# Second attention of a hybrid decoder layer: a branch product in two query halves, its last input kept on chip, and three moved or merged steps

## The chip, the cores and the metric

The kernel runs on one core of a Trainium2 chip. The metric is the device time of one execution in microseconds (us); the kernel before takes 1424.58 us, the median of three runs between 1424.15 and 1425.3. TensorE is called PE here, VectorE DVE, ScalarE ACT, GpSimd POOL, and SP is the engine whose queue issues nearly all DMAs of this kernel.

## What is computed

One layer with three parallel token mixers over 512 tokens and a model width of 1024:

```python
h = rms_norm(x);  u = h @ w_in                       # one combined projection
y_a = dsa_mixer(...)                                 # first attention (16 heads)
y_b = nsa_mixer(...)                                 # second attention (16 heads, two groups of 8)
y_c = ssd_mixer(...)                                 # state space mixer (2048 wide)
gates = sigmoid(mg)                                  # three gates per token and column
mix = gates[0]*(y_a @ w_br_dsa) + gates[1]*(y_b @ w_br_nsa) + gates[2]*(y_c @ w_br_ssd)
x = x + mix @ w_out
x = x + square(relu(rms_norm(x) @ w_ff1)) @ w_ff2
```

The second attention adds, for each query, a window part and a selected-blocks part (and a compressed part), each with its own softmax and gate. Everything is float32. A float32 product is computed as three matmuls of rounded operands: each operand is split into a high half (a rounded copy, made on ACT) and a low half (the operand less its high half, made on POOL or DVE), and `mm3` (L352) issues high x high, low x high and high x low.

## The kernel before

Two Python generators write the program. `main` (L1513) holds the attention and the state space mixer, `filler` (L577) holds the dense projections. `main` yields a cost, and the loop at its end lets `filler` emit about as much work; `main`'s instructions are emitted with a priority that is 4000 ahead (`HM`, L36). The order of each engine's queue is set when the program is built, from these priorities. So the attention's steps stand first wherever they are ready, and the projections fill TensorE between them. A generator that yields `None` waits for a flag in `done`.

The second attention (`nsa_units`, L987) runs 8 pairs of a query block b (128 queries) and a head group g in the order (3,0) (0,0) (2,0) (1,0) (3,1) (2,1) (1,1) (0,1). Each pair has two sets j of four heads and for each set a window unit and a selected-blocks unit, 32 units in all. A unit's scores are made by `a1` (L788) and exponentiated on ACT; `a2` (L812) takes 1/sum, multiplies it by the gate (L818) and scales four p tiles with it, three on DVE (L823) and the fourth on POOL (L821); `b1` (L825) transposes the p tiles, splits them and multiplies them with V into `pv`. At the end of a set ACT copies the lower part of `pv` (L856), DVE adds the two parts (L857), and SP writes the 256 rows by 128 queries to `y_d["b"]` in DRAM (L858).

`branches` (L1247) is the last part of the filler that runs beside this attention: the passes a0, a1, c0, c1, b0, b1 in this order. Each pass multiplies some row tiles of a mixer's result (128 rows by 512 queries, four in a0, a1, b0 and b1, eight in c0 and c1) with a branch weight, for eight column tiles m of the output. For a pass `load_y` (L709) reads each row tile from DRAM into a staging buffer (two exist), makes the high half on ACT (L715) and the low half on POOL (L716; in b1 on DVE), into a pool of four buffers: pool A for a0, B for a1 and b0, both for c0 and c1, and a pool C for b1. For each m, `load_g` (L1253) reads the gate tile, 128 by 512, 256 KB, into one of two buffers named `gld`; the product goes to one of two PSUM banks named `pj`; DVE multiplies it with the gate in place (L1329, or L1331 in c, where L1319 first multiplies the gate with a norm factor; in a0 L1326 writes `mix` at once); then `mix` takes it up, on POOL (L1332) in a1, c0, c1 and b0 and on DVE in b1. A gate buffer is free only after that addition, so a gate tile is loaded into it after the addition for m-2.

b1 is the last pass: rows 512 to 1023 of `y_d["b"]`, that is group g=1 of all four query blocks. It starts when the last unit is being emitted (flag `nsa5`), opens two column tiles with the two row tiles of set j=0, and waits for `nsa`, the attention's end, for the two row tiles of set j=1. After each column tile of b1, ACT and DVE make the halves `mixh`, `mixl` (L1334, L1335), on which the output product `w_out` (pass "wo") rests. Weights come in chunks of up to 128 by 1024 through `WS` (L104): three raw buffers (`RAWB`), six split ones (`NS`); the weight of a0, a1, b0 and b1 is one chunk of 128 by 512 for each m, that of c0 and c1 128 by 1024.

## Time and profile before

| | |
|---|---|
| median of three runs | 1424.58 us (1424.15 to 1425.3) |
| profiled execution, its own time | 1425.82 us |
| its span, first to last instruction | 1424.1 us |
| TensorE matmul busy | 1365.5 us (96%) |
| TensorE weight load busy | 1126.1 us (79%) |
| VectorE busy | 1044.6 us (73%) |
| ScalarE busy | 712.6 us (50%) |
| GpSimd busy | 347.0 us (24%) |
| mean granted TensorE clock | 0.987 |

The second attention runs from about 600 to 1010 us, the passes a0 to b1 from 749 to 1039 us, the output product from 1039 us on. A TensorE busy share near 100% doesn't mean that the engine is at its peak, since matmuls overlap; the spacing of starts is read beside it.

### The profile page before, as it was taken

The page shows a single profiled execution, that of the slowest core. Times are in us where ns is not written, and L with a number is a line of the kernel's source. Part 1 is how long each engine was busy: PE and PEld are TensorE (multiplying, and loading weights), DVE is VectorE, ACT ScalarE, POOL GpSimd, SP SyncE. Part 2 cuts the span into 40 slices and gives each one's busy share as a digit, 9 for nine tenths or more (in the row PEclk, how much of TensorE's full clock was granted, in tenths as well). Part 3 has the DMA queues.
Part 4 walks back from the last instruction along what each step waited for, and adds up shares of the span by engine and source line. Part 5 has one row for each costly group of instructions (what it writes and reads, how often), then busy time and mean ns, then how long its engine had stood idle before and what let it go on. Part 6 is the DMA issues. An engine that isn't in the chain of part 4 may idle for free.

```text
span 1424.1 us, 19720 instructions
## 1 busy us (share of the span) xinstructions
PE 1365.5 (96%) x6760; PEld 1126.1 (79%) x6760; DVE 1044.6 (73%) x1959; ACT 712.6 (50%) x1433; POOL 347.0 (24%) x294
## 2 busy tenths in 40 slices
PE   5989899999999999999999999999799999999998
PEld 4878688888877877788888867787579888888887
DVE  4599966798977665468568898888655777869841
ACT  5445245677666566455555544646433444443420
POOL 5454201111046576202003533524100000000000
PEclk9999899999999999999999999999999999999999
DMA  6236465544576778844326743424464433241221
GB/s 204 73 102 139 130 189 144 137 113 125 133 224 190 215 202 223 232 139 122 96 79 193 228 134 87 136 67 126 158 212 127 126 111 110 87 136 45 67 89 52
DMA packets 232097, 195.92 MB, mean 138 GB/s; under 512 B 17200, under 2 KB 183484, under 8 KB 231996
## 3 DMA queue, kind: packets, MB, share of 16 engines
q1 hardware_dynamic: 226524, 183.12, 44.3%
q0 software_dynamic: 4608, 8.39, 2.2%
q10 hardware_dynamic: 864, 3.15, 0.6%
q8 instruction: 53, 0.87, 0.3%
q14 instruction: 48, 0.39, 0.1%
HBM read 157.85 MB, written 36.77 MB: 137 GB/s over the span
## 4 chain that ended last, share of the span: by engine, by line
PE 71%; DVE 10%; DMA 7%; issue 4%; ACT 4%; POOL 2%; SPq 2%; DVEq 0%; ACTq 0%; POOLq 0%
PE pj L365 17%; PE pj L366 17%; PE pj L367 16%; PE sc L366 3%; PE sc L367 3%; PE sc L365 3%; PE pT L837 2%; PE sc L802 2%; PE sc L801 2%; PE pv L850 2%; PE pv L849 2%; DVE wlo L159 1%; DMA gld<-g_d 1%; SPq L525 1%; DMA E<-ac_d 1%
## 5 line engine op out<-in xcount | busy, mean ns | idle before, releaser
L158 ACT ACTIVATE whi<-wraw 128x1024 fp32r<-128x1024 f32 (+3 forms) x188 | 181.7, 975 | 210.8 <-PE pj L366 124.3
L159 DVE TENSOR_TENSOR wlo<-wraw,whi 128x1024 fp32r<-128x1024 f32 (+1 forms) x164 | 194.5, 1188 | 77.4 <-ACT whi L158 75.6
L365 PE MATMUL pj<-hTh,whi 128*128 128x512 f32 x384 | 154.9, 403 | 0.2 <-DVE cacc L732 0.2
L367 PE MATMUL pj<-hTh,wlo 128*128 128x512 f32 x384 | 153.5, 400 | 0.0
L366 PE MATMUL pj<-hTl,whi 128*128 128x512 f32 x384 | 153.3, 399 | 0.0
L365 PE MATMUL pj<-whi,hTh 128*128 128x512 f32 (+2 forms) x352 | 141.6, 404 | 8.3 <-DVE stk L435 3.2
L810 ACT ACTIVATE p<-p,nb,rs 128x256 f32<-128x256 f32 (+3 forms) x192 | 123.2, 645 | 50.6 <-DVE nb L808 50.6
L366 PE MATMUL pj<-wlo,hTh 128*128 128x512 f32 (+2 forms) x352 | 140.0, 398 | 0.8 <-POOL wlo L159 0.8
L367 PE MATMUL pj<-whi,hTl 128*128 128x512 f32 (+2 forms) x352 | 138.5, 394 | 0.0
L365 PE MATMUL pj<-yh,whi 128*128 128x512 f32 x256 | 103.0, 406 | 9.4 <-ACT yh L715 7.7
L366 PE MATMUL pj<-yl,whi 128*128 128x512 f32 x256 | 102.2, 399 | 0.4 <-DVE yl L716 0.4
L367 PE MATMUL pj<-yh,wlo 128*128 128x512 f32 x256 | 101.9, 399 | 0.0
L366 PE MATMUL pj<-h2l,whi 128*128 128x512 f32 (+1 forms) x256 | 96.3, 376 | 0.0
L367 PE MATMUL pj<-h2h,wlo 128*128 128x512 f32 (+1 forms) x256 | 96.2, 376 | 0.0
L365 PE MATMUL pj<-h2h,whi 128*128 128x512 f32 (+1 forms) x256 | 96.1, 376 | 0.0
L821 POOL TENSOR_TENSOR p<-p,rc 128x256 f32<-128x256 f32 (+3 forms) x48 | 38.2, 795 | 219.7 <-DVE rc L816 63.2
L365 PEld LDWEIGHTS pj<-whi,hTh 128*128 128x128 f32 x352 | 68.3, 194 | 22.5 <-issue 6.4
L365 PEld LDWEIGHTS pj<-hTh,whi 128*128 128x128 f32 x384 | 72.3, 188 | 16.4 <-issue 1.7
L367 PEld LDWEIGHTS pj<-hTh,wlo 128*128 128x128 f32 x384 | 72.2, 188 | 15.2 <-issue 1.2
L366 PEld LDWEIGHTS pj<-hTl,whi 128*128 128x128 f32 x384 | 72.3, 188 | 15.0 <-issue 1.7
L841 ACT ACTIVATE pth<-pT 128x512 fp32r<-128x512 f32 x95 | 55.0, 593 | 56.8 <-PE pT L837 54.8
L366 PEld LDWEIGHTS pj<-wlo,hTh 128*128 128x128 f32 x352 | 68.4, 194 | 14.9 <-issue 2.2
(357 smaller groups left out, 3372.9 us busy)
## 6 DMA issues: line engine op xcount, KB each, us to landing
wraw<-in_w_in_dram SPq DMA_DIRECT2D x84, 512.0 KB, 4.5
wraw<-in_w_ff_dram SPq DMA_DIRECT2D x40, 512.0 KB, 4.1
gld<-g_d SPq DMA_DIRECT2D x48, 256.0 KB, 3.3
qd<-in_w_ff_dram SPq DMA_DIRECT2D x24, 512.0 KB, 3.9
q_d<-qev SPq DMA_DIRECT2D x128, 64.0 KB, 2.6
qu<-q_d POOLq DMA_DIRECT2D x32, 256.0 KB, 3.7
E<-ac_d SPq DMA_DIRECT2D x16, 512.0 KB, 4.9
wraw<-in_w_br_ssd_dram SPq DMA_DIRECT2D x16, 512.0 KB, 3.8
```

What stands on the lines that cost most here:

```text
L158: act.activation(hi[:, :m], r[:, :m], AF.Copy)
L159: (pool if i < NP else dve).tensor_tensor(lo[:, :m], r[:, :m], f(hi[:, :m]), op=ALU.subtract)
L365: pe.matmul(o, lh, rh, start=first, stop=False)
L366: pe.matmul(o, lh, rl, start=False, stop=False)
L367: pe.matmul(o, ll, rh, start=False, stop=last)
L801: pe.matmul(s_[:, h % w, :n], u.q[:, h], kh[:, :n], start=True, stop=False)
L802: pe.matmul(s_[:, h % w, :n], u.q[:, h], kl[:, :n], start=False, stop=True)
L810: act.activation(u.p[h][:, :n], u.p[h][:, :n], AF.Exp, bias=u.nb[:, h:h + 1], scale=rs8[:, u.b, u.h0 + h:u.h0 + h + 1], accum_out=u.sm[:, ...
L821: pool.tensor_tensor(u.p[h][:, :n], u.p[h][:, :n], bc(rc[:, h:h + 1], [128, n]), op=ALU.mult)
L837: pe.transpose(pt[:, h], u.p[h][:, kb * 128:kb * 128 + 128], ident)
L841: act.activation(ph, ptf, AF.Copy)
L849: pe.matmul(o, vk, ph0, start=st, stop=False)
```

## The change

The branch weight of a is used in one pass of eight row tiles, with 128 by 1024 chunks. The weight of b comes in chunks of four row tiles by 256 columns (two m). The pass b1 takes only queries 256 to 511 (blocks 2 and 3), and starts while the seventh pair runs (flag `nsah`); a new pass b2 takes queries 0 to 255 with the same weights, which stay in their buffers. Queries 0 to 127 of b2 are the last pair's result: it is put from PSUM straight into b2's operand tiles `YH`, `YL` and goes to no DRAM. All low halves of y are made on DVE, and the fourth p tile of the second attention is scaled on ACT. The diff, cut to its core:

```diff
-SPL = {"a0": 1, "a1": 1, "c0": 1, "c1": 1, "b0": 1, "b1": 0}
...
-    P["br_a0"] = [plan_ch(A["w_br_dsa"], D, 128 * m, 0, 4) for m in range(8)]
-    P["br_a1"] = [plan_ch(A["w_br_dsa"], D, 128 * m, 4, 4) for m in range(8)]
+    P["br_a0"] = [plan_ch(A["w_br_dsa"], D, 128 * m) for m in range(8)]
...
-    P["br_b0"] = [plan_ch(A["w_br_nsa"], D, 128 * m, 0, 4) for m in range(8)]
-    P["br_b1"] = [plan_ch(A["w_br_nsa"], D, 128 * m, 4, 4) for m in range(8)]
+    for br, k0 in (("b0", 0), ("b1", 4)):
+        P["br_" + br] = [ws.add([(wcols(A["w_br_nsa"], D, k0, 4, 256 * m, 256), 256)], 4, 256) for m in range(4)]
...
-        (pool if SPL[br] else dve).tensor_tensor(l_, yr, f(h_), op=ALU.subtract)
+        dve.tensor_tensor(l_, yr, f(h_), op=ALU.subtract)
...
             if h == 3:
-                pool.tensor_tensor(u.p[h][:, :n], u.p[h][:, :n], bc(rc[:, h:h + 1], [128, n]), op=ALU.mult)
+                if u.gate is not None:
+                    act.activation(u.p[h][:, :n], u.p[h][:, :n], AF.Copy, scale=rc[:, h:h + 1])
+                else:
+                    pool.tensor_tensor(u.p[h][:, :n], u.p[h][:, :n], bc(rc[:, h:h + 1], [128, n]), op=ALU.mult)
...
+        if u.last and u.direct is not None:
+            yt = at.tile([64, 4, 128], F32, name="yt", bufs=YTB)
+            act.activation(yt.rearrange("p a b -> p (a b)"), o[64:128], AF.Copy)
+            yr, h_, l_ = u.direct
...
+            for e in range(2):
+                dve.tensor_tensor(yr[64 * e:64 * e + 64], o4[:, :, e], t4[:, :, e], op=ALU.add)
+            act.activation(h_, yr, AF.Copy)
+            dve.tensor_tensor(l_, yr, f(h_), op=ALU.subtract)
...
+        def half(g):
+            yield from g
+            done.add("nsah")
+
+        def direct(u, j):
+            done.add(f"nsaq{j}")
+            yield "yC"
+            u.direct = YC[j]
...
+                    if i == 7 and kind == "s":
+                        u.load = lambda u=u, j=j: direct(u, j)
+                    elif i == 6 and j == 1 and kind == "s":
+                        u.load = lambda i=i: half(cont(i + 1, cmp_c))
...
+        BR = ("a0", "c0", "c1", "b0", "b1", "b2")
+        KS = {"a0": (0, 8), "c0": (0, 8), "c1": (8, 8), "b0": (0, 4), "b1": (4, 4), "b2": (4, 4)}
+        COLS = {"b1": (256, 512), "b2": (0, 256)}
...
-                g_ = bp.tile([128, S], F32, name="gld", bufs=2)
-                nc.sync.dma_start(g_, g_d[(bi * 8 + m) * 128:(bi * 8 + m + 1) * 128])
+                c0, c1 = COLS.get(br, (0, S))
+                g_ = bp.tile([128, S], F32, name="gld", bufs=2)[:, :c1 - c0]
+                nc.sync.dma_start(g_, g_d[(bi * 8 + m) * 128:(bi * 8 + m + 1) * 128, c0:c1])
...
             if br == "a0":
-                Y = ya
-                Y1 = load("a1", range(4, 8), "B")
+                Y = ya + load("a0", range(4, 8), "B")
...
+            elif br == "b1":
+                while "nsah" not in done:
+                    yield None
+                yc = popen("yC")
+                YH = yc.tile([128, 4, S], F32R, name="yh2")
+                YL = yc.tile([128, 4, S], F32R, name="yl2")
+                load_b(256, 512)
...
+                yr = gp.tile([128, 2, 2, 128], F32, name="yr", tag="gt", bufs=TG)
...
+            elif br == "b2":
+                while "nsaq0" not in done:
+                    yield None
+                load_b(128, 256)
+                while "nsaq1" not in done:
+                    yield None
...
+                    if half:
+                        while "nsa" not in done:
+                            yield None
                     for m in range(BH):
...
                         for k in (2 * half, 2 * half + 1):
-                            mm3(pp[m], wh[:, k, :], wl[:, k, :], yh[k], yl[k], k == 0, k == 3)
+                            mm3(pp[m][:, :256], wh[:, k, ms], wl[:, k, ms], YH[:, k, 0:256], YL[:, k, 0:256], k == 0, k == 3)
...
+                            if k % 2:
+                                if k == 3 and m % 2 and br != "b1":
+                                    ws.free(wi)
+                                yield 6 * (c1 - c0) / 2.37
...
-                (dve if br == "b1" else pool).tensor_tensor(mix[:, m], mix[:, m], th, op=ALU.add)
-                if br == "b1":
+                (dve if br in ("b1", "b2") else pool).tensor_tensor(mx, mx, th, op=ALU.add)
+                if br == "b2":
                     act.activation(mixh[:, m], mix[:, m], AF.Copy, scale=0.5)
                     dve.scalar_tensor_tensor(mixl[:, m], mix[:, m], 0.5, f(mixh[:, m]), op0=ALU.mult, op1=ALU.subtract)
```

`load_b` reads the four row tiles of one query range in one or two DMAs and splits them on ACT and DVE. `mixh` and `mixl` are made in b2 for all 512 queries.

## Rows read from the trace of the kernel before

**Rows 1.** Busy time by stretch: PE, PEld, DVE, ACT, POOL (instructions), granted clock, DMA share, GB/s.
```profile
750.00:1001.00 251.00, 242.89 (x1239) 197.63 (x1238) 216.34 (x502) 134.80 (x302) 100.56 (x82) 1.00 0.47 139
1005.00:1020.00 15.00, 7.45 (x22) 4.92 (x23) 5.30 (x7) 2.77 (x5) 1.67 (x1) 0.77 0.35 107
1095.00:1110.00 15.00, 15.00 (x128) 15.00 (x127) 6.44 (x8) 5.83 (x8) 0.00 (x0) 1.00 0.81 287
```

**Rows 2.** Who TensorE waited for, 750 to 1001 us (largest): total, times, longest.
```profile
PE sc L801 <- DVE mx L803: 2.9, 6, 1.3
```

**Rows 3.** Timeline of TensorE at the attention's end: start, us, instruction, [idle before, releaser].
```profile
1001.15 0.39 PE L367 MATMUL pj<-yh,wlo 128*128 128x512 f32 x1
1016.35 1.22 PE L365 MATMUL pj<-yh,whi 128*128 128x512 f32 x2 [7.18 <-ACT yh L715]
1018.23 0.63 PE L365 MATMUL pj<-yh,whi 128*128 128x512 f32 x1
1018.65 0.63 PE L366 MATMUL pj<-yl,whi 128*128 128x512 f32 x1
1039.18 0.39 PE L367 MATMUL pj<-yh,wlo 128*128 128x512 f32 x1
```

**Rows 4.** The chain that ended last, 1003 to 1025 us: start, us, what.
```profile
1010.54 2.45 DMA yb_d<-yt
...
1013.01 2.64 DMA yr<-yb_d
...
1015.67 0.64 ACT yh L715
```

**Rows 5.** Gate tiles on two timelines: two SP issues, then three DVE instructions of one buffer.
```profile
1007.17 0.95 SPq L1258 DMA_DIRECT2D gld<-g_d  x1
...
1029.03 0.32 SPq L1258 DMA_DIRECT2D gld<-g_d  x1
...
1026.58 0.69 DVE L1329 SCALAR_TENSOR_TENSOR gld<-gld,pj 128x512 f32<-128x512 f32 x1 [0.86 <-DMA gld<-g_d]
...
1028.32 0.69 DVE L1332 TENSOR_TENSOR mixf<-mixf,gld 128x512 f32<-128x512 f32 x1
...
1033.04 0.68 DVE L1329 SCALAR_TENSOR_TENSOR gld<-gld,pj 128x512 f32<-128x512 f32 x1
```

**Rows 6.** A 256-column product on DVE, both operands in SBUF (timeline).
```profile
828.16 0.40 DVE L943 TENSOR_TENSOR pgt<-ct,gate 128x256 f32<-128x256 f32 x1
```

**Rows 7.** Groups of instructions, whole span: busy, mean ns, idle before and its releasers.
```profile
L716 POOL TENSOR_TENSOR yl<-yr,yh 128x512 fp32r<-128x512 f32 x28 | 40.1, 1441 | 26.6 <-ACT yh L715 24.8 <-DMA yr<-ya_d 1.6 <-DMA gld<-g_d 0.2
L1200 ACT ACTIVATE yev<-pT,gcol 128x128 f32<-128x128 f32 x64 | 17.9, 361 | 7.4 <-issue 7.1 <-PE pT L1197 0.3
L1334 ACT ACTIVATE mixh<-mixf 128x512 fp32r<-128x512 f32 x8 | 5.1, 633 | 8.9 <-DVE mixf L1332 8.9
```

**Rows 8.** Landing times by tile: `gld` in 1018 to 1050, `gld` in 980 to 1012, `yt`.
```profile
DMA to landing us min/median/max: 3.3/4.1/4.5
...
DMA to landing us min/median/max: 2.6/3.1/3.9
...
DMA to landing us min/median/max: 2.4/2.4/4.5
```

**Rows 9.** Timelines, DVE beside POOL: L818 beside L1332, L716 beside L1332, L818 alone.
```profile
809.30 1.27 DVE L818 TENSOR_TENSOR rc<-rc,gate 128x4 f32<-128x4 f32 x1
...
809.26 1.28 POOL L1332 TENSOR_TENSOR mixf<-mixf,gld 128x512 f32<-128x512 f32 x1 [3.66 <-DVE rc L816]
...
1005.92 1.77 DVE L716 TENSOR_TENSOR yl<-yr,yh 128x512 fp32r<-128x512 f32 x1
...
1005.47 1.67 POOL L1332 TENSOR_TENSOR mixf<-mixf,gld 128x512 f32<-128x512 f32 x1 [2.16 <-DVE gld L1329]
...
831.88 0.16 DVE L818 TENSOR_TENSOR rc<-rc,gate 128x4 f32<-128x4 f32 x1
```

**Rows 10.** ACT timeline: the last of the four row tiles of a1, into pool B.
```profile
764.41 0.63 ACT L715 ACTIVATE yh<-yr 128x512 fp32r<-128x512 f32 x1 [3.07 <-DMA yr<-ya_d]
```

More of the change, by code (lines that the diff above doesn't have):

```diff
@@ L895, in dsa_units @@
                 u.b, u.h0, u.k, u.v = b, 4 * hb, K["d"], V["d"]
-                u.gate, u.first, u.last, u.pre, u.load = None, True, True, None, None
+                u.gate, u.first, u.last, u.pre, u.load, u.direct = None, True, True, None, None, None
                 u.ydst = y_dst("a", 4 * hb, b)
@@ L1010, in att2 @@
             yield from g
-        def nsa5():
-            done.add("nsa5")
-            yield 0
+        def half(g):
[5 more added lines that the diff above has]
+            u.direct = YC[j]
         def both(i):
@@ L1251, in branches @@
         th_ = {}
+        BR = ("a0", "c0", "c1", "b0", "b1", "b2")
+        KS = {"a0": (0, 8), "c0": (0, 8), "c1": (8, 8), "b0": (0, 4), "b1": (4, 4), "b2": (4, 4)}
+        COLS = {"b1": (256, 512), "b2": (0, 256)}
+        seq = [(br, m) for br in BR for m in range(8)]
+        ypools["B"] = popen("yB")
         def load_g(n):
@@ L1276, in branches @@
             k0, nk = KS[br]
+            c0, c1 = COLS.get(br, (0, S))
+            pp = {}
             if br == "a0":
-                Y = ya
-                Y1 = load("a1", range(4, 8), "B")
-            elif br == "a1":
-                Y = Y1
-            elif br == "b1":
-                while "nsa5" not in done:
-                    yield None
-                ypools["C"] = popen("yC")
-                Y = load(br, (4, 5), "C")
-                while "nsa" not in done:
-                    yield None
-                Y += load(br, (6, 7), "C")
-                mp = popen("mix", side="right")
-                mixh = mp.tile([128, KT, S], F32R, name="mixh")
-                mixl = mp.tile([128, KT, S], F32R, name="mixl")
+                Y = ya + load("a0", range(4, 8), "B")
             elif br == "b0":
                 Y = load(br, range(4), "B")
-            else:
-                Y = load(br, range(k0, k0 + 4), "A") + load(br, range(k0 + 4, k0 + 8), "B")
-            yh = [y[0] for y in Y]
-            yl = [y[1] for y in Y]
-            pp = {}
-            if br == "b1":
+            elif br == "b1":
[5 more added lines that the diff above has]
+                load_b(256, 512)
+                Y = [(YH[:, k], YL[:, k]) for k in range(4)]
+                yr = gp.tile([128, 2, 2, 128], F32, name="yr", tag="gt", bufs=TG)
+                for j in range(2):
+                    YC.append((yr[:, j], YH[:, 2 * j:2 * j + 2, 0:128], YL[:, 2 * j:2 * j + 2, 0:128]))
+                done.add("yC")
+            elif br == "b2":
[4 more added lines that the diff above has]
+                    yield None
                 load_g(8 * bi)
@@ L1305, in branches @@
                 for half in range(2):
+                    if half:
+                        while "nsa" not in done:
+                            yield None
                     for m in range(BH):
-                        wi = P["br_b1"][m]
-                        wh, wl = ws.get(wi)
+                        wh, wl = ws.get(P["br_b1"][m // 2])
+                        ms = slice(128 * (m % 2), 128 * (m % 2) + 128)
                         for k in (2 * half, 2 * half + 1):
-                            mm3(pp[m], wh[:, k, :], wl[:, k, :], yh[k], yl[k], k == 0, k == 3)
-                        if half:
-                            ws.free(wi)
-                        yield 6 * 216
+                            mm3(pp[m][:, :256], wh[:, k, ms], wl[:, k, ms], YH[:, k, 0:256], YL[:, k, 0:256], k == 0, k == 3)
+                        if half and m % 2:
+                            ws.free(P["br_b1"][m // 2])
+                        yield 6 * 108
+                mp = popen("mix", side="right")
+                mixh = mp.tile([128, KT, S], F32R, name="mixh")
+                mixl = mp.tile([128, KT, S], F32R, name="mixl")
+            else:
+                Y = load(br, range(k0, k0 + 4), "A") + load(br, range(k0 + 4, k0 + 8), "B")
+            yh = [y[0] for y in Y]
+            yl = [y[1] for y in Y]
             for m in range(8):
```

38 lines of the change are left out of this document (26 added, 12 removed).

## The prediction

> **What bounds the kernel now.** I read four views, in this order. The busy time by stretch comes first. From 750 to 1001 us, where the second attention and the branch passes share TensorE, it is idle for 251.00 - 242.89 = 8.1 us [rows 1]; the largest named part of this is a wait for the row maxima on DVE, 2.9 us [rows 2]. From 1005 to 1020 us it is busy for only 7.45 of 15 us, and the granted clock averages 0.77 [rows 1]. So the stretch to look at is the end of the attention.
>
> The timeline of TensorE and the chain that ended last show what is there. The last b0 product starts at 1001.15, the last b1 product at 1039.18 [rows 3]: 38.0 us. Before the second half of b1 TensorE stands for 7.18 us [rows 3], and the chain says why: SP writes the last result to DRAM from 1010.54 (2.45 us), reads it back from 1013.01 (2.64 us), and ACT makes the high half at 1015.67 [rows 4]. After this idle stretch 512-column matmuls follow each other at 0.42 us (1018.23 to 1018.65) [rows 3], which is the lower of the clock's two levels (1.2 GHz); at the upper one a 256-column matmul takes 15/128 = 0.117 us [rows 1], so a 512-column one about 0.23. Some eight matmuls run slow, which costs 1.5 us. The work in the 38 us is 96 products of 512 columns, 96 x 0.234 = 22.5 us, and about 2 us of attention. So about 13.5 us are lost, 8.7 of them in this hole.
>
> The last view is that of the gate tiles, since b1's tail is not bound by TensorE alone. The DVE product with a gate tile starts at 1026.58, after a wait of 0.86 us for that tile; the addition that frees the buffer starts at 1028.32; SP issues the next load at 1029.03; the next product in the same buffer starts at 1033.04 [rows 5]. That is 6.46 us for one turn of a buffer, and two buffers serve two column tiles in a turn: 3.2 us for each column tile, above the 12 x 0.234 = 2.8 us that TensorE needs. The reader should keep this loop in mind, as the change makes it turn sixteen times where it turned eight.
>
> **The change part by part.** *The result kept on chip.* It removes two writes of 128 KB, the reads of row tiles k=4..7 as whole rows, and the chain from 1010.54 to 1015.67, 5.1 us. It puts in two additions on 64 partitions (0.40 to 0.68 us each; I take 0.40 from the 256-column row [rows 6]) and a high half of 256 columns (0.4 us, between 0.361 for 128 and 0.633 for 512 columns [rows 7]). TensorE could go on at about 1011.2 in place of 1016.35, and b1's other half can be run before that. The hole of 7.18 us goes and, with it, the idle stretch ahead of the lower clock: 8.7 us. What is late next is the gate loop.
>
> *Two query halves.* TensorE's work stays: 192 x 0.117 = 22.5 us. Each half has eight column tiles, and each of them a gate load of half the size, a product and an addition of 256 columns. So the loop has sixteen steps. One turn of a buffer is: landing, 4.1 us with a 512 KB weight load just ahead of it, 3.1 us in the stretch before [rows 8]; for 128 KB the trace shows only writes (median 2.4 us [rows 8]). I take 2.9: half of the steps behind a weight load (4.1 less some 0.5), half without (2.4). Then 0.40 for the product and 0.40 for the addition [rows 6], against 0.69 each; between them now 1028.32 - 1027.27 = 1.05 us of weight split, and as about 7 splits fall on 16 steps, 0.45; and 0.05 to the issue. The turn is 4.2 us. Bounds: 3.35 (landing 2.4, gap 0.1) and 5.4 (landing 4.1, as if size did not count).
>
> The odd buffer sets the end. It is free when b0's last addition on POOL ends, and SP issues its next load at 1007.17 [rows 5]; landing 3.0, so its first product is at 1010.2. Six turns later, 1010.2 + 25.2 = 1035.4, the product for m=5 of b2 starts, which frees the PSUM bank for m=7; 0.4 + 12 x 0.117 = 1.8 us later TensorE has done b2: 1037.2, against 1039.4 (1039.18 and its own 0.23). The tail is worth 2.2 us (bounds: a turn of 3.35 gives 1032.1 and 7.3 us; 5.4 gives 1044.4 and a loss of 5.0). The DVE halves of `mix` then end some 6 us after TensorE's b2; the first two token blocks of w_out cover that, as they did in b1.
>
> The Trainium skill, page "DMA: Bandwidth & Descriptors", section "Anatomy of one DMA", speaks against this part: a DMA has a fixed cost of about 2 us, on top of which the bytes come, so that halving a tile saves little of its landing. By it a load would go from 3.1 to about 2.8 us and a turn would be an estimated 4.3 us, a tail worth 1.6 us.
>
> *Low halves on DVE.* 28 instructions leave POOL (40.1 us [rows 7]) and come to DVE at 0.68 us: 19 us more. a in one pass takes away 8 gate products of 0.69 us [rows 5], 8 additions on POOL and 8 gate loads; larger weight chunks save some 3 us of splits. On the other side, DVE loses time beside POOL: a product of 4 columns takes 1.27 us and ends with POOL's 1.28 us addition, where the same one takes 0.16 alone; a low half takes 1.77 us beside POOL's 1.67 [rows 9]. POOL's work in 750 to 1001 us falls from 100.56 us [rows 1] to about 40: 34 us of low halves, 13 of additions and 16 of p tiles go. DVE ends about level in busy time, but what stood in the attention's chain (L818, the p tiles) gets shorter. I take 2.5 us of the 8.1 idle; bounds 0 and 5.
>
> The Trainium skill, page "SBUF — State Buffer", section "Who interferes with whom", says that a DVE instruction with two SBUF inputs and a GpSimd one that reads SBUF exclude each other for a whole instruction. The two pairs agree. It speaks against this part too: a low half has two SBUF inputs, and 24 additions stay on POOL.
>
> *Fourth p tile on ACT.* 32 instructions go from POOL to ACT, at 0.36 (128 columns) to 0.63 us (512) [rows 7], about 16 us on an engine that is busy for 134.80 of 251 us [rows 1]. They run beside DVE's three tiles and end no later, so they cost nothing; if ACT is late, the first transposes are, by at most one such instruction a unit. Behind it in ACT's queue wait the copies of the transposed tiles.
>
> *a in one pass.* The first column tiles now need all eight row tiles at once. In the kernel before, the last one's high half starts at 764.41, after ACT waited 3.07 us for it [rows 10], 15 us after pass a began. Two column tiles can run four row tiles ahead, and the attention fills in. I take 1.0 us lost; bounds 0 and 4. The same holds for c0, whose row tiles must now wait for the end of a for all eight buffers; in c0 to c1 this is so already.
>
> **The sum.** Tail 2.2, relief of DVE 2.5, pass a -1.0: 3.7 us off the profiled execution's 1425.82, whose span is 1424.1. It lies 1.2 above the median; off the median it gives 1420.9.
>
> **The rivals.** *The gate loop turns fast* (3.35 us, or the DVE order puts both products together): tail 7.3, relief 2.5, no loss in a: 1424.6 - 9.0 = 1415.6. For it: 128 KB lands in 2.4 us at best, and fewer splits lie between. *The gate loop turns slowly, so the kernel is slower:* the place is b1 and b2, the price six turns; from 27.4/6 = 4.57 us a turn the tail gains nothing. At 5.4 it loses 5.0, with 1.5 of relief: 1428.1. For it: 4.1 us landing behind weight loads, which is also when w_out's come. *Low halves hold up DVE:* POOL waited 24.8 us for high halves [rows 7], ACT for the DMAs ahead of these. In DVE's queue this wait would stand ahead of the attention's steps. A third of it, 8 us, and the gains above: 1429. Against it: DVE is busy for 216.34 of 251 us and mostly comes late to such a step anyway. *The change doesn't do what it says:* the round trip through DRAM goes, but the last gate tile comes as late as before (a turn near 4.57): 1424.6 less relief of 1.5, 1423, and with a reordered queue up to 1427.
>
> **How the numbers follow.** A measurement of this kernel can tell about 0.2% from no change, 2.8 us. Forecast, 1417.5 to 1421.7: 0.30. Fast loop, 1409 to 1417.5: 0.25. Nothing to be told, 1421.7 to 1427.4: 0.22. Slow loop, to 1430: 0.15. Low halves in DVE's queue: 0.08. So faster 0.55, same 0.22, slower 0.23. The range goes from 1410 to 1429.
>
> **What would show it.** In the profile after: no yb_d write and read in the last 10 us of the attention, and no idle stretch above 3 us on TensorE; the clock at 1.00 there; DVE's gate products in b1 and b2 waiting for `gld`, their distance in one buffer near 4.2 us; w_out starting near 1037; L818 near 0.16 us more often; TensorE idle in 750 to 1001 below 8. I am wrong if the gate tiles land with time to spare, if DVE waits for high halves, or if the attention itself ends at another time by more than 5 us.

## The result, and the profile after

The changed kernel takes 1408.86 us, the median of four runs (1405.88 to 1410.4), beside 1424.37 us for the kernel before (1422.21 to 1425.3): a ratio of 0.9873 with a 95% interval of 0.984 to 0.9905, 15.5 us less. On another chip the same pair gave 0.9879 (0.9842 to 0.9917). The prediction had the sign, but 3.7 us in place of 15.5, and a range that ended at 1410.

The profiled execution took 1410.33 us, its span is 1408.6 us. VectorE is busy for 1022.7 us of it, ScalarE for 725.3 and GpSimd for 267.1. The line numbers of the changed kernel are shifted: the low half of y is L714, the fourth p tile L820, the gate product of b L1383, the addition L1386, the halves of the result kept on chip L862 and L863. In the kernel before, some definitions stand at other lines than the text on it gives: `mm3` at L364, `filler` at L593, `main` at L1509, `nsa_units` at L993, `WS` at L122.

Busy time by stretch, columns as in [rows 1], and under it two groups of instructions of 750 to 1001 us (busy, mean ns, idle before):

```profile
750.00:1001.00 251.00, 244.62 (x1287) 205.74 (x1286) 205.88 (x522) 147.43 (x319) 40.12 (x31) 0.99 0.45 136
1005.00:1020.00 15.00, 12.73 (x96) 11.66 (x95) 11.82 (x24) 6.16 (x9) 0.00 (x0) 1.00 0.34 104
```
```profile
L714 DVE TENSOR_TENSOR yl<-yr,yh 128x512 fp32r<-128x512 f32 x24 | 16.2, 686 | 1.0 <-ACT yh L713 1.0
L820 ACT ACTIVATE p<-p,rc 128x256 f32<-128x256 f32 (+3 forms) x20 | 11.2, 560 | 5.4 <-DVE rc L816 5.4
```

GpSimd's work between 750 and 1001 us falls from 100.56 to 40.12 us, as predicted; VectorE's falls by 10 us although it took over the low halves, and waits only 1.0 us for high halves. At the attention's end the clock stays at 1.00, where it was 0.77. The timeline of TensorE there, to be held against [rows 3]:

```profile
1007.58 0.39 PE L851 MATMUL pv<-ptl,v_s 128*128 128x512 f32 x1
...
1009.99 0.50 PE L363 MATMUL pj<-yh,whi 128*128 128x256 f32 x2 [0.58 <-ACT yh L862]
...
1024.18 0.28 PE L365 MATMUL pj<-yh,wlo 128*128 128x256 f32 x1
1024.30 0.40 PE L363 MATMUL pj<-whi,mixh 128*128 128x512 f32 x1
```

And the same two places, the attention's last product and the start of the output product, in the kernel before:

```profile
1008.78 0.39 PE L850 MATMUL pv<-ptl,v_s 128*128 128x512 f32 x1
...
1039.48 0.47 PE L365 MATMUL pj<-whi,mixh 128*128 128x512 f32 x1
```

The idle stretch of 7.18 us is 0.58 us now, and the output product starts at 1024.30 in place of 1039.48, 15 us earlier: by here the whole gain has been made. But the attention's last product is only 1.2 us earlier (1007.58 against 1008.78), because 11 us of b1's work now lie before it. So the time came from two places, and to tell them apart I use one account throughout. **Lost time** is worked out from TensorE's timeline: from each matmul's start to the next start, less what that matmul takes at the upper clock with nothing in its way (0.2275 us for 512 columns, 0.1185 for 256, and so on). It is summed from 600 us on, up to b1 (where the last 22 us of branch work begin) and from there to the last branch matmul. Each number is from one profile; against the measured times the sums are right to about 5 us, in one case (10) to 7. The differences between kernels hardly hang on what is taken for the smallest matmuls, but the level does: with 0.06 us for 128 columns the kernel before loses 46 us up to b1, with 0.11 us 20, and the changed kernel loses 7 to 9 us less in each case. All runs, each ratio against runs of the kernel before that were made beside it:

| kernel | ratio to before, 95% interval | lost up to b1, us | lost from b1 on, us | lowest clock of the five 10 us stretches from 985 to 1035 |
|---|---|---|---|---|
| before | 1 | 35.6 | 13.1 | 0.76 |
| changed | 0.9873 (0.984 to 0.9905) | 27.0 | 7.5 | 1.00 |
| 1: p tile on GpSimd | 1.0000 (0.9981 to 1.0018) | 32.2 | 16.0 | 0.73 |
| 2: low halves on GpSimd | 0.9932 (0.9904 to 0.9959) | 30.2 | 7.0 | 1.00 |
| 3: both on GpSimd | 0.9997 (0.9978 to 1.0016) | 39.2 | 9.5 | 1.00 |
| 4: spare work on GpSimd | 0.9941 (0.9923 to 0.9958) | 33.4 | 8.9 | 1.00 |
| 5: as 1, order of changed | 0.9912 (0.9877 to 0.9946) | 27.7 | 7.4 | 1.00 |
| 6: changed, order of 1 | 0.9950 (0.9924 to 0.9976) | 27.3 | 14.5 | 0.70 |
| 7: as 3, order of changed | 0.9907 (0.9878 to 0.9936) | 29.9 | 7.7 | 1.00 |
| 8: a in two passes | 0.9920 (0.9896 to 0.9944) | 24.7 | 15.3 | 0.79 |
| 9: as 6, late product | 0.9916 (0.9884 to 0.9949) | 25.6 | 14.5 | 0.70 |
| 10: before, late product | 0.9976 (0.9958 to 0.9994) | 38.3 | 13.9 | 0.77 |
| 11: before, both moves, order kept | 0.9975 (0.9954 to 0.9995) | 32.3 | 12.9 | 0.62 |
| 12: changed, late product | 0.9898 (0.9875 to 0.9922) | 28.2 | 7.4 | 1.00 |
| 13: as 6, attention ahead | 1.0070 (1.0044 to 1.0097) | 43.7 | 15.7 | 0.78 |
| 14: no halves | 0.9918 (0.9888 to 0.9948) | 24.8 | 16.0 | 0.70 |
| 15: changed again | 0.9879 (0.9842 to 0.9917) | 25.7 | 7.4 | 1.00 |
| 16: gate tiles in pairs | 0.9857 (0.9833 to 0.9881) | 26.5 | 6.9 | 1.00 |
| 17: read halves later | 0.9860 (0.9839 to 0.9882) | 23.0 | 7.3 | 1.00 |
| 18: 16 and 17 | 0.9862 (0.9844 to 0.9880) | 22.8 | 7.7 | 0.83 |

0.1% is 1.4 us. By lost time the change gains 8.6 us up to b1 and 5.6 us from b1 on.

### The profile page after: what moved, and what is told of

The parts are those of the page before. It is cut to its first block, busy times and chain, and to the rows that moved or that the text cites. A ratio compares the mean times of both kernels' runs of the same rounds, so it can differ in the third digit from the quotient of the medians.

```text
span 1408.6 us, 19755 instructions
## 1 busy us (share of the span) xinstructions
PE 1360.3 (97%) x6856; PEld 1133.4 (80%) x6856; DVE 1022.7 (73%) x1982; ACT 725.3 (51%) x1450; POOL 267.1 (19%) x226
## 4 chain that ended last, share of the span: by engine, by line
PE 74%; DVE 10%; DMA 7%; issue 3%; ACT 2%; POOL 2%; SPq 1%; DVEq 0%; POOLq 0%; ACTq 0%
PE pj L363 17%; PE pj L364 17%; PE pj L365 17%; PE sc L363 3%; PE sc L364 3%; PE sc L365 3%; PE pT L838 3%; PE sc L800 2%; PE sc L799 2%; PE pv L850 2%; PE pv L851 2%; DMA wraw<-in_w_in_dram 2%; DMA bcx<-BC_d 1%; DVE wlo L158 1%; DVE mask L776 1%
## 5 line engine op out<-in xcount | busy, mean ns | idle before, releaser
L157 ACT ACTIVATE whi<-wraw 128x1024 fp32r<-128x1024 f32 (+2 forms) x172 | 179.0, 1048 | 200.6 <-PE pj L364 118.9
L158 DVE TENSOR_TENSOR wlo<-wraw,whi 128x1024 fp32r<-128x1024 f32 x148 | 188.9, 1279 | 77.8 <-ACT whi L157 77.0
L364 PE MATMUL pj<-hTl,whi 128*128 128x512 f32 x384 | 153.6, 400 | 0.0
L364 PE MATMUL pj<-wlo,hTh 128*128 128x512 f32 (+2 forms) x352 | 140.5, 400 | 0.4 <-POOL wlo L158 0.4
L363 PE MATMUL pj<-yh,whi 128*128 128x512 f32 (+1 forms) x288 | 107.0, 379 | 8.7 <-DVE gld L1383 7.7
L364 PE MATMUL pj<-yl,whi 128*128 128x512 f32 (+1 forms) x288 | 107.6, 374 | 0.0
L365 PE MATMUL pj<-yh,wlo 128*128 128x512 f32 (+1 forms) x288 | 107.5, 373 | 0.0
L364 PE MATMUL pj<-h2l,whi 128*128 128x512 f32 (+1 forms) x256 | 96.3, 376 | 0.0
L893 POOL DMA_DIRECT2D qu<-q_d x32 | 18.3, 574 | 356.0 <-PE sc L800 265.9
L364 PEld LDWEIGHTS pj<-hTl,whi 128*128 128x128 f32 x384 | 72.3, 188 | 14.8 <-issue 1.4
L364 PEld LDWEIGHTS pj<-wlo,hTh 128*128 128x128 f32 x352 | 68.5, 195 | 14.5 <-issue 2.2
```

The source lines that it names most:

```text
L157: act.activation(hi[:, :m], r[:, :m], AF.Copy)
L158: (pool if i < NP else dve).tensor_tensor(lo[:, :m], r[:, :m], f(hi[:, :m]), op=ALU.subtract)
L363: pe.matmul(o, lh, rh, start=first, stop=False)
L364: pe.matmul(o, lh, rl, start=False, stop=False)
L365: pe.matmul(o, ll, rh, start=False, stop=last)
```

## The experiments

**Undo the engine moves.** The prediction put both at 2.5 us. The diffs are against the changed kernel and shortened.

```diff
 # 1 (and 3): the fourth p tile
-                    act.activation(u.p[h][:, :n], u.p[h][:, :n], AF.Copy, scale=rc[:, h:h + 1])
+                    pool.tensor_tensor(u.p[h][:, :n], u.p[h][:, :n], bc(rc[:, h:h + 1], [128, n]), op=ALU.mult)
 # 2 (and 3): the low half in load_y
-        dve.tensor_tensor(l_, yr, f(h_), op=ALU.subtract)
+        pool.tensor_tensor(l_, yr, f(h_), op=ALU.subtract)
 # 4: after each of the two, with s_ a scratch tile of 256 columns, in parts
+            pool.tensor_tensor(s_[:, :c1], caus[:, c:c + c1], bc(x, [128, c1]), op=ALU.mult)
```

> The changed kernel with the fourth p tile back on GpSimd; all else as changed. Before: 1424.4 us, changed: 1408.9, 15.5 between them. By a running account of TensorE's lost time (the spacing of its starts less the work), 9.2 of the 15 us are gained from 810 to 930 us, some 7 in 990 to 1020, and 2 are given back in 930 to 990. Theory 1, relief: GpSimd's instructions slow VectorE's (the small product took 1.27 us beside GpSimd and 0.16 alone), and 32 p tiles are a third of the GpSimd work that went: about 3 of the 9 us come back, 1412. Theory 2, GpSimd's order: the p tile stood in GpSimd's queue behind additions that wait for gate tiles, so it was late in the attention's chain: most of the 9 us come back, 1416 to 1418. Theory 3, neither: the 9 us come from the one pass of a and the gate loads that went with it: 1409.

> The changed kernel with the 28 low halves of y back on GpSimd (28 x 1.44 = 40 us of its work); p tile on ScalarE as changed. Theory 1, relief by less GpSimd work beside VectorE: two thirds of the 9 us come back, 1414 to 1415. Theory 2, GpSimd's order: low halves on GpSimd delay nothing of the attention once the p tile is gone from that queue, so 1409 to 1411. Theory 3, the one pass of a: 1409, or below, as 19 us leave VectorE.

> The changed kernel with both, p tile and low halves, back on GpSimd; the one pass of a, the two query halves and the result kept on chip stay. Theories 1 and 2: all of the 9 us come back, 1416 to 1419, and TensorE's lost time from 810 to 930 is near 16 again. Theory 3: 1409 to 1411. If it is above 1420, the tail's gain hangs on the relief too.

> The changed kernel, p tile on ScalarE and low halves on VectorE, with spare work put on GpSimd at the same places: for each of the 32 p tiles and the 28 low halves a product of as many columns of a constant, written to a scratch tile in parts of 256 columns and read by nobody (it starts when the real one could). It tells theory 1 from theory 2: by theory 1 (GpSimd beside VectorE slows VectorE, whatever the work is for) the time goes back as in the kernel with both on GpSimd, 1416 to 1419, and the small product on VectorE is above 0.3 us on average again; by theory 2 (what counts is that an operand came late from GpSimd's queue) it stays at 1409 to 1411 with VectorE's instructions longer all the same.

Measured: 1.0000, 0.9932, 0.9997 and 0.9941 (1425.75, 1415.3, 1426.63 and 1420.03 us beside 1427.05). The p tile alone takes back everything, far above what any of the three theories gave it, and taking the low halves back as well costs nothing more. The kernel with spare work that nobody reads is 0.7% slower than the changed one. VectorE's small steps of the attention take longer in it (750 to 1001 us, spare work first, then changed):

```profile
L823 DVE TENSOR_TENSOR rc<-rc,gate 128x4 f32<-128x4 f32 x19 | 7.4, 395 | 0.1
L813 DVE SCALAR_TENSOR_TENSOR nb<-mx,rs 128x4 f32<-128x4 f32 x19 | 5.5, 288 | 0.1
```
```profile
L816 DVE TENSOR_TENSOR rc<-rc,gate 128x4 f32<-128x4 f32 x20 | 5.7, 286 | 0.3
L806 DVE SCALAR_TENSOR_TENSOR nb<-mx,rs 128x4 f32<-128x4 f32 x21 | 4.1, 201 | 0.0
```

Yet a tenth of a microsecond in each such step doesn't make 18 us of 32 p tiles. The lists of the queues gave the reason: the program that orders them when the kernel is built goes by its own costs, so each of these four kernels, that with the spare work too, had another order of its matmuls and on VectorE and ScalarE. An undone edit alone can't be priced that way.

**Hold the order.** The next kernels pin every queue to a given sequence of instructions, by an edge of issue order (without a wait) from each instruction to its forerunner on the same engine, in short:

```diff
+    for i in sequence:                      # the sequence of another kernel, instruction by instruction
+        k = str(i.engine)
+        if k in last:
+            tc.add_manual_dep(i, last[k], NoSync)
+        last[k] = i.name
```

> The kernel with the p tile back on GpSimd took all of the gain away (1.000 of before), far more than relief gives; but the order in which each queue holds its instructions is made by a scheduling program that goes by its own costs, and it made another order there: of TensorE's 6652 matmuls 1594 stand at another place than in the changed kernel, of VectorE's 1738 instructions 515. So here the p tile is on GpSimd again and every queue is held to the order of the changed kernel, instruction by instruction; only the 32 p tiles change their queue. Theory A, the engine: GpSimd's p tile is slower (1.44 us and up to 1.8 for 512 columns against 0.72) and slows VectorE beside it, whatever the order: 0.998 to 1.002 of before again. Theory B, the order: most of the loss was the other order, and the engine costs only what 32 later p tiles cost where TensorE has no other work: 0.988 to 0.992 of before. In between, the shares are read from the two runs.

> The counterpart: the changed kernel, p tile on ScalarE, all queues held to the order that was made for the p tile on GpSimd. Theory A, the engine: 0.987 to 0.990 of before, the order matters little. Theory B, the order: 0.996 to 1.001 of before, although every instruction is that of the changed kernel.

> p tile and low halves of y both on GpSimd, all queues held to the order of the changed kernel. With its own order this kernel was at 1.000 of before. Theory A: 0.998 to 1.003 again, or above, as GpSimd has 60 us more work at places that were not chosen for it. Theory B: 0.990 to 0.994: what is then lost against the changed kernel (0.987) is the price of the engine alone, which I put at 2.5 us in the prediction, that is 0.989.

> The kernel before, every queue in its own order, with the p tile on ScalarE and the low halves on VectorE (the two engine moves alone; one pass of a, halves and on-chip result left out). At the changed kernel's order the two moves were worth 0.0034 of before, 4.8 us. If that is the price of the engines whatever the order, 0.996 to 0.997 here; the prediction's 2.5 us is 0.998. If a low half on VectorE holds up its queue (a rival of the prediction), 1.000 to 1.004.

Measured: 0.9912, 0.9950, 0.9907 and 0.9975. Theory B holds in the main: with the order of the changed kernel the p tile on GpSimd costs 0.3 to 0.4%, not 1.2%, and the low halves nothing beside it; the intervals of 5 and 7 overlap with the changed kernel's. At the order of before the two moves gain 0.25%, 3.5 us (interval 0.7 to 6.6). At the order made for kernel 1 the p tile alone is worth 0.5%, 7 us: kernels 1 and 6 have the same order and differ in the p tile alone, and their intervals lie apart (1.0000 and 0.9950). So the price of an engine move hangs on the order too. The changed kernel's own instructions in the order made for kernel 1 are 0.7 to 0.8% slower (0.9950 against 0.9873 and 0.9879), again with intervals apart. Up to b1 both orders lose the same, 27.3 and 27.0 us; the difference lies behind, 14.5 against 7.5. The stretches of 1005 to 1025 us, kernel 6 and then changed:

```profile
1005.00:1010.00 5.00, 1.94 (x12) 1.27 (x11) 3.48 (x16) 4.81 (x18) 0.00 (x0) 0.89 0.27 78
1010.00:1015.00 5.00, 5.00 (x20) 4.39 (x21) 2.66 (x6) 1.79 (x4) 0.00 (x0) 0.50 0.00 0
1015.00:1020.00 5.00, 2.93 (x14) 2.32 (x14) 1.26 (x3) 1.01 (x2) 0.00 (x0) 0.84 0.00 0
1020.00:1025.00 5.00, 4.84 (x31) 4.64 (x30) 4.60 (x9) 2.47 (x4) 0.00 (x0) 0.74 0.26 73
```
```profile
1005.00:1010.00 5.00, 4.42 (x35) 4.04 (x33) 3.62 (x9) 1.01 (x2) 0.00 (x0) 1.00 0.33 99
1010.00:1015.00 5.00, 4.96 (x36) 4.46 (x36) 3.73 (x7) 2.22 (x4) 0.00 (x0) 1.00 0.20 62
1015.00:1020.00 5.00, 3.36 (x26) 3.16 (x27) 4.47 (x9) 2.93 (x4) 0.00 (x0) 1.00 0.49 151
1020.00:1025.00 5.00, 3.69 (x27) 3.36 (x27) 4.43 (x10) 2.14 (x5) 0.00 (x0) 1.00 0.67 245
```

A busy share alone misleads here: from 1010 to 1015 us kernel 6 is busy for 5.00 of 5 us with 20 matmuls at a granted clock of 0.50 (1.2 GHz), the changed kernel for 4.96 with 36. What stands ahead of the drop in kernel 6:

```profile
1005.77 0.40 PE L851 MATMUL pv<-ptl,v_s 128*128 128x512 f32 x1
1008.06 0.72 PE L838 MATMUL pF<-ident,p 128*128 128x128 f32 x3 [1.89 <-DVE p L824]
1009.95 0.48 PE L838 MATMUL pF<-ident,p 128*128 128x128 f32 x1 [1.17 <-DVE p L824]
...
1018.42 0.50 PE L363 MATMUL pj<-yh,whi 128*128 128x256 f32 x2 [2.07 <-ACT yh L862]
```

From 1005.77 to 1012.5 us the attention's last steps run with no branch product between them, TensorE waits for VectorE's p tiles, and the clock falls. The on-chip result doesn't prevent it: the wait for its high half is 2.07 us.

**What in the order costs it?** Two readings were tried. The first is that VectorE waits for gate tiles with the attention's steps behind it in its queue. Kernels 9, 10 and 12 move the 16 products (gate + 1) x scale of c in VectorE's queue, nothing else:

```diff
-  ... L1360 of tile m ... (2 to 45 instructions) ... L1385 of tile m     # VectorE's queue
+  ... (2 to 45 instructions) ... L1360 of tile m, L1385 of tile m
```

> The order alone cost 0.77% (0.995 against 0.987 of before, same instructions on the same engines). Theory C on what in the order costs: VectorE's queue holds the first product of each c gate tile, (gate + 1) x scale, 2 to 45 places ahead of the second one, which takes the matmul's result; where that place comes before the tile has landed, VectorE waits with the attention's steps queued behind. It waited 18.5 us for these tiles in the order made for the p tile on GpSimd, 2.5 us in the changed kernel's, 10.4 us before. Here that slow order again, every queue as it was, but the 16 first products moved in VectorE's queue to right ahead of their second ones. By theory C the waits of 18.5 us go to below 3 and the time to 0.988 to 0.990. Rival: the waits are a sign and not a cause (the loss sits in the order of TensorE's matmuls or of SP's loads, which stay): 0.994 to 0.996.

> The kernel before, every queue in its own order, with only the 16 first products of the c gate tiles moved in VectorE's queue to right ahead of their second ones. It waited 10.4 us for these tiles. Theory C: it gains 3 to 6 us, 0.996 to 0.998 of before, with the changed kernel's other edits left out; if it gains nothing, the waits of before were beside other work, and the order cost something else there.

> The changed kernel in its own order with the 16 first products of the c gate tiles moved to right ahead of their second ones. It waited 2.5 us for them. Theory C: at most 1 us to gain, and each move puts 0.69 us behind the matmul's end, so 0.986 to 0.989 of before. If it comes out at 0.992 or above, the late place has a price of its own, which then also stands in the two kernels beside it. It is at the same time the candidate for a faster kernel.

Measured: 0.9916, 0.9976 and 0.9898. The waits of VectorE, 740 to 1000 us (total, times, longest), kernel 6 and then 9:

```profile
DVE gld L1360 <- DMA gld<-g_d: 18.5, 9, 5.3
DVE p L801 <- PE sc L800: 10.5, 8, 2.7
DVE rc L814 <- ACT p L808: 7.5, 10, 1.6
```
```profile
DVE rc L814 <- ACT p L808: 17.7, 15, 2.9
DVE p L801 <- PE sc L800: 13.2, 10, 2.8
```

18.5 us of waiting for gate tiles are gone, and 13 us come up again under the next names; lost time falls by 1.7 us (41.8 to 40.1), the time by 0.34% with intervals that overlap. So the wait was mostly a sign: what it cost is not clear of noise. In the kernel before, the measured gain (0.24%) is not borne out by its one profile, whose lost time rose; that stays unexplained.

> What the slow order has that the changed kernel's has not, counted in TensorE's queue: behind the first 256-column product of b1 stand 52 attention matmuls there, 16 in the changed kernel; the attention is up to 86 branch matmuls later throughout. In the traces the lost time up to b1 is the same in both (27.3 and 27.0 us from 600 us on), and from b1 on it is 14.5 against 7.5. Theory D: the order costs what the attention's steps cost when they are left for the end with no branch product to run beside them. Here the slow order again, with the attention's instructions (scores, softmax, transposes, products with v, on every queue, in their own sequence) moved ahead from the first c product on, so that 23 are left behind b1's first product; all other sequences stay. Theory D: lost time from b1 on 7 to 9 us, time 0.987 to 0.990 of before. If the order costs something else (loads on SP, gate products on VectorE), 0.994 to 0.997, as without the move.

The second reading, theory D, is that attention steps left for the end have no branch product beside them. The edit of 13: in kernel 6's sequence the attention's instructions on all queues are moved ahead by up to 86 branch matmuls, rising from the first c product on. Measured: 1.0070, slower than the kernel before. Theory D as a rule has fallen: 23 attention matmuls were left behind b1's first product in place of 52, and the time from b1 on lost as much (15.7 us), while 16 us more were lost ahead of it. Why is not shown: VectorE waited 16.3 us for exponentials there, but in kernel 9, which lost 25.6 us up to b1, it waited 17.7. Kernel 4 speaks against the theory too: 48 matmuls left, and 8.9 us lost. What the table does show is that each kernel which kept the clock at 1.00 lost 6.9 to 9.5 us from b1 on, and each whose clock fell at the attention's end 12.9 to 16.0. In 18 it fell only behind the attention, after a stall of 1.98 us ahead of b2's last column tile, with 7.7 us lost. The halves and the on-chip result don't decide it: kernels 1, 6, 8, 9 and 13 have both and lose 14.5 to 16.0 us there, no less than before (13.1). Which feature of an order leads to the one or the other stays open.

**The one pass of a and the halves.**

```diff
 # 8, against the changed kernel
-    P["br_a0"] = [plan_ch(A["w_br_dsa"], D, 128 * m) for m in range(8)]
+    P["br_a0"] = [plan_ch(A["w_br_dsa"], D, 128 * m, 0, 4) for m in range(8)]
+    P["br_a1"] = [plan_ch(A["w_br_dsa"], D, 128 * m, 4, 4) for m in range(8)]
 ...
 # 14, against the kernel before: the two engine moves, and a in one pass
 ...
-                Y = ya
-                Y1 = load("a1", range(4, 8), "B")
+                Y = ya + load("a0", range(4, 8), "B")
```

> The changed kernel with branch a in two passes of four row tiles, as before (eight gate products, eight additions on GpSimd and eight gate loads more), in the order that is made for it. Theory of the prediction: one pass costs 1.0 us (bounds 0 and 4), so 1405 to 1409 against 1408.9, 0.985 to 0.987 of before. Theory 3 (one pass gives the gain of the middle): 1414 to 1418, 0.993 to 0.996. If the order alone moves such a kernel by many us, any value from 0.985 to 1.000 may come, and it then says little about the pass itself.

> The kernel before with the p tile on ScalarE, the low halves on VectorE and a in one pass; without the query halves and the result kept on chip, in the order that is made for it. The two engine moves at the order of before gave 0.9975. Prediction: one pass costs 1.0 us, so 0.998; what is then missing to the changed kernel's 0.987 is the end of b (5 to 6 us by lost time from b1 on: 13.1 before, 7.5 changed) and the order. If it comes out at 0.990 or below, the halves give little and the order of the middle most; the lost time from b1 on should be 13 to 14 us in any case, since the read back from DRAM stays.

> The changed kernel as it is, beside the other three: 0.987 of before, with an interval that can be compared with theirs on the same chip.

Measured: 0.9920, 0.9918 and 0.9879. Kernel 8 loses less up to b1 than the changed kernel (24.7 against 27.0 us) and 15.3 behind it: no price of the pass can be read from it, only another order. Kernel 14 is the important one. Without halves it is already 0.8% faster than before, and up to b1 it loses 24.8 us, the least but for 8, 17 and 18. Kernel 11, with the same engine moves in the order of before, loses 32.3. Of what 14 adds to 11, the one pass is not needed for this, since 8 has two and loses 24.7, and the halves, which 8 has, are not needed either, since 14 has none. What 8 and 14 have in common against 11 is a new order. Its hole at the attention's end is still there:

```profile
1000.00:1005.00 5.00, 0.00 (x0) 0.00 (x0) 0.00 (x0) 0.17 (x1) 0.00 (x0) 0.58 0.48 131
1005.00:1010.00 5.00, 4.49 (x11) 3.48 (x12) 1.34 (x2) 1.33 (x3) 0.00 (x0) 0.50 0.00 0
```

**The loop of gate buffers, and a stall of the new kernel.** Kernel 16 (order of the changed kernel) puts two gate tiles of b1 or b2 into one buffer, so that four can be in flight; kernel 17 moves b1's first read halves in two queues; 18 does both.

```diff
 # 16
 ...
+                if br in COLS:
+                    for e in range(2):
+                        th_[n + e] = g_[:, 256 * e:256 * e + 256]
+                        nc.sync.dma_start(th_[n + e], g_d[(bi * 8 + m + e) * 128:(bi * 8 + m + e + 1) * 128, c0:c1])
+                    return
 ...
 # 17, VectorE's queue (ScalarE's is left out)
-  L1298 L1298  L1383 L868 L1383 L801 L801
+  L1383 L868 L1383 L801 L801  L1298 L1298
```

> The changed kernel in its own order with one edit: in b1 and b2 each of the two gate buffers of 512 columns holds two gate tiles of 256 columns (two loads into its halves), so four tiles are in flight in place of two. The lost time from b1 on is 7.5 us in the changed kernel, and TensorE's waits for gate products in it are 0.63, 0.87, 0.90, 0.78 and 1.31 us, 4.5 in all. If the loop of gate buffers sets the end, as the prediction had it, these waits go and 3 to 4.5 us with them: 0.984 to 0.985. If the loop is not what ends it (the loads stand behind others in SP's queue, or the attention's own steps are late), it stays at 0.987.

> The changed kernel in its own order, with one move. Its largest stall (3.2 us in one profile, 3.0 in another) comes at 966 to 970 us: the two low halves of b1's first rows (256 columns) stand in VectorE's queue ahead of the first two gate products of b0 and of the evaluation of the scores; they wait for ScalarE, which waits 5.2 us for their reads from DRAM, and b1 needs them some 20 us later. TensorE stands, and the lost time from 960 to 990 us is 5.1 to 6.8 us. Here these two low halves stand behind two gate products, one addition of a result and two score evaluations, and their high halves behind one copy on ScalarE; nothing else moves. If the place in the queue is the cause, the stall goes and 3 to 5 us with it: 0.984 to 0.985 of before against 0.987 to 0.988. If the gate products were late for another reason, 0.987 to 0.988 and the stall stays under another name.

> Both moves on the changed kernel: gate tiles of 256 columns in pairs (0.986 alone) and the read halves of b1 later in the queues. If they add, 0.982 to 0.984 of before, some 4 to 7 us below the changed kernel; if the tail only takes up what the middle gives, as with the pairs alone, where lost time from b1 on fell by 0.5 us of the 4.5 looked for, 0.984 to 0.986.

Measured: 0.9857, 0.9860 and 0.9862 (1408.09, 1408.06 and 1408.05 us beside 1427.37 and 1427.03). VectorE's waits for gate tiles, 985 to 1025 us, changed again (15) and then pairs (16):

```profile
DVE gld L1383 <- DMA gld<-g_d: 4.0, 7, 1.0
```
```profile
DVE gld L1388 <- DMA gld<-g_d: 1.4, 2, 0.9
```

2.6 us of waiting are gone and lost time from b1 on goes from 7.4 only to 6.9: the number of buffers alone is not what ends the tail. But the largest wait of TensorE in kernel 16's tail still ends on a gate tile (VectorE, SP twice, VectorE, TensorE):

```profile
1010.77 0.42 DVE L1391 TENSOR_TENSOR mixf<-mixf,gld 128x256 f32<-128x256 f32 x1
...
1015.70 0.38 SPq L141 DMA_DIRECT2D wraw<-in_w_out_dram  x1
1016.13 0.93 SPq L1287 DMA_DIRECT2D gld<-g_d  x2
...
1020.15 0.81 DVE L1388 SCALAR_TENSOR_TENSOR gld<-gld,pj 128x256 f32<-128x256 f32 x2 [0.54 <-DMA gld<-g_d]
...
1020.63 0.39 PE L363 MATMUL pj<-yh,whi 128*128 128x256 f32 x1 [1.94 <-DVE gld L1388]
```

The first of these loads goes into a buffer that has been free since the addition ended at 1011.19. It goes out only at 1016.13, because a weight load stands ahead of it in SP's queue, whose order was held, and that one waited for VectorE's weight split (L158, until 1015.67). So four tiles were not in flight when it mattered: the limit went from the buffers to SP's queue, and no run moves the loads there.

The stall that kernel 17 aims at, in the timelines of kernel 15 (VectorE, ScalarE, TensorE):

```profile
963.99 0.69 DVE L1298 TENSOR_TENSOR yl<-yr,yh 128x512 fp32r<-128x512 f32 x1 [3.94 <-ACT yh L1297]
965.30 0.69 DVE L1298 TENSOR_TENSOR yl<-yr,yh 128x512 fp32r<-128x512 f32 x1 [0.62 <-ACT yh L1297]
965.91 0.68 DVE L1383 SCALAR_TENSOR_TENSOR gld<-gld,pj 128x512 f32<-128x512 f32 x1
...
963.33 0.63 ACT L1297 ACTIVATE yh<-yr 128x512 fp32r<-128x512 f32 x1 [5.18 <-DMA yr<-yb_d]
...
966.64 0.50 PE L363 MATMUL pj<-yh,whi 128*128 128x512 f32 x1 [3.02 <-DVE gld L1383]
```

A low half that b1 needs some 20 us later waits in VectorE's queue for a read from DRAM, and the gate product that frees a PSUM bank stands behind it. With the two moved behind it, the stretch of 960 to 975 us, kernel 15 and then 17:

```profile
960.00:975.00 15.00, 11.98 (x58) 9.90 (x58) 8.99 (x26) 7.26 (x22) 5.13 (x4) 1.00 0.53 166
```
```profile
960.00:975.00 15.00, 15.00 (x77) 12.58 (x76) 10.89 (x25) 6.00 (x13) 7.75 (x4) 1.00 0.54 168
```

The stall is gone, so its cause is shown; lost time up to b1 falls from 25.7 to 23.0 us in one profile each. In the times 16, 17 and 18 lie 0.1 to 0.2% below the changed kernel, within the intervals: all three beat the kernel before, and none is shown to beat the changed one. That the two gains add, which would have given 0.982 to 0.984, did not come true.

## Why the prediction was wrong

**The sum had no term for the order; that is the step that failed.** It priced each edit with all else in its place, but every queue is ordered anew when the kernel is built, and that alone moved the same instructions by 0.7 to 0.8%, 10 to 11 us (6). From before to changed: 0.25% for the engine moves with the order held (11), a further 0.57% with the one pass of a and a new order (14), and 0.42% with the halves, the on-chip result and again a new order (0.9876, the mean of both measurements), each to some 0.3%. The middle term, 8 us, is in no line of the sum; the nearest bound was that of the relief, 5 us. That it is the order's and not the pass's is an inference from the lost time of 8, 11 and 14; no run has the one pass with the order of before.

**Relief of VectorE, 2.5 us (bounds 0 and 5): right in size at the order of before, and not a constant.** 3.5 us there, 4 to 5 at that of the changed kernel (0.9907 and 0.9912 against 0.9873 and 0.9879, intervals overlapping), but 7 us for the p tile alone at the order of kernel 1. How much of it is a faster VectorE, and how much a p tile that comes earlier, no run separates: the kernel with spare work (4) had an order of its own. The cap of 8.1 us that I took from TensorE's idle time [rows 1] was no bound at all for more than this: by spacing the kernel before loses 35.6 us from 600 us to b1, where it is idle for 8.1, so most of it lies between matmuls that the busy time counts as work. The Trainium skill, page "SBUF — State Buffer", section "Who interferes with whom", says that a VectorE instruction with two SBUF inputs contends with a GpSimd one that reads SBUF. With the order held the means of two such steps between 750 and 1001 us agree in the main. The product of 1/sum and gate goes from 345 to 299 ns from before to 11, from 310 to 244 from 1 to 6, and from 354 to 286 from 5 to the changed kernel. The step that makes `nb` goes from 398 to 337, from 232 to 174, and, against the rest, from 180 to 201.

**Tail, 2.2 us (bounds -5.0 and 7.3): right in sign, 5.6 by lost time, and in part by luck.** The hole went, as said, and with it the lower clock, but only in this order: with the same halves and on-chip result kernels 1, 6, 8, 9 and 13 gain nothing there. And I let the gate loop set the end. Its start was wrong: I kept SP's issue at 1007.17 [rows 5], and b0 ended 10 us earlier, so that the first gate product of b1 came at 995.69. Its turn in b1 was 3.7 us, not 4.2 (starts in one buffer at 995.69, 1000.01, 1003.28 and 1006.77), since tiles of half the size landed in 2.2 us (median) where I had 2.9. With twice the buffers the last gate tiles came late all the same, behind weight loads in SP's queue (16). The figures of the Trainium skill, page "DMA: Bandwidth & Descriptors", section "Anatomy of one DMA" (2.0 us and the bytes, stated there for the GpSimd path), give an estimated 2.3 us for such a tile, which the 2.2 us bear out; the 3.1 and 4.1 us of whole tiles [rows 8] lie above the 2.6 that they give as an estimate for 256 KB, and my estimate carried that surplus over. The turn that I worked out by that page, 4.3 us, doesn't follow from the 2.8 us beside it: the same terms give 4.1.

**Pass a, -1.0 us: not settled.** Neither 8 nor 14 tells it from the order in the times; by lost time up to b1 two passes and one come out alike (24.7 and 24.8).

**The rivals.** The fast loop gave 1415.6, though its terms, 7.3 and 2.5, make 9.8 and so 1414.8; its turn of 3.35 us is nearer to the measured 3.7 than my 4.2, but TensorE did not go by the turn alone (16). The slow loop did not show: within b1 and b2 turns lay between 3.3 and 4.3 us but for one of 6.0 in b2. "Low halves hold up VectorE" was put at 8 us against 28 low halves; these wait 1.3 us in all, but two new ones, of b1's first read, do just that for 3 us (17). That the change does what it says is shown by the timeline of after.

**The list of what would show it.** Round trip gone: yes. No idle stretch above 3 us at the end and the clock at 1.00: yes. Small product near 0.16 us more often: only from 345 to 286 ns on average. TensorE idle below 8 us in 750 to 1001: 6.4. The output product near 1037: 1024.3, and there the account of one edit after the other broke. The attention's end, which was not to move by more than 5 us: 1.2 us earlier.

## What to carry to other kernels

Where a program orders the queues, an edit is worth its own price plus that of the order it brings, and the second can be the larger: here the same instructions differed by 0.7% between two orders, while the engine moves were worth 0.25 to 0.5% with the order held. Price an edit with the order held, and measure an undone edit both ways, before a cause is named. A wait that is taken away can come back under another name, so read the lost time of the engine that bounds and not the wait, and read the granted clock beside the busy time.

## What the runs showed of the hardware

TensorE at the lower clock looks fully busy: 5.00 of 5 us with 20 matmuls at 0.50. With idle stretches of 1 to 3 us at the attention's end the clock fell in kernels 1, 6, 8, 9 and 13, in kernel 6 to 0.50 for some ten us, but not in kernels 3 and 4 with stretches of 1.25 and 1.68 us; a single stall of 3 us had both outcomes, 0.89 over 960 to 975 us in one profile of the changed kernel and 1.00 in the other. Loads of 128 KB landed in 2.2 us (2.1 to 3.3) in the tail of the changed kernel, those of 256 KB in 4.0 us there before.
